# Seven-product W_O in the middle block, with the next block's operands spread over three weight stages, and column sums by transposition

## The chip, the cores and the metric

The kernel runs on one core of one Trainium2 chip. The metric is the device time of one execution in microseconds (us), lower is better. PE is TensorE (matrix products), DVE is VectorE, ACT is ScalarE, POOL is GpSimd and SP is SyncE; SP and POOL issue the DMAs.

## The reference

It is one layer of a hybrid streaming model in float32, for a prompt of 2048 tokens and a decode batch of 64 tokens with a model width D of 1024. Cut to what matters here:

```
h = rms_norm(x, g_pre);  proj = h @ w_in                       # ten outputs of width 1024
vA,bA,cA,zA,q,f,iv,zB,gA,gB = split(proj)
yA = (silu(zA) * bA * conv3(cA * vA)) @ w_a_out                # path A
yB = (norm(gated_linear_attention(q, f, iv)) * silu(zB)) @ w_b_out   # path B, 8 heads
merged = sigmoid(gA) * yA + sigmoid(gB) * yB
out = merged @ w_o
x = x + rms_norm(out, g_post)
x = x + (p @ w_ple_proj) * sigmoid(rms_norm(x, g_ple) @ w_ple_gate)
```

`rms_norm` divides by the root of the mean square over the 1024 features of a token.

## The kernel before, in words

**Blocks.** All 2112 tokens lie in the columns, features in the 128 partitions. Three blocks of 704 tokens (first, middle, last) are worked one after the other, each as two halves of 352 columns, so nearly every matmul has a moving operand of 128x352. Each float32 product is made of three matmuls: weights and activations are split into a high and a low part (`split`: ACT casts the high part, DVE subtracts it for the low part), and high x high, high x low and low x high are added up in PSUM.

**Products.** A product with 2x2 sub-blocks (two column blocks of weights, two token halves) takes 8 sub-products when done plainly. Most stages use seven instead (Strassen's way in Winograd's form): sums S1 to S4 of weight blocks and T1 to T4 of activation blocks are built first, and seven sub-products are combined. `sgroup` does seven products for one pair of weight columns. `in_turn` does one product after the other for all four pairs `g` of a weight matrix: 7 products x 4 pairs x 12 matmuls, 336 in all; while product `n` runs, `prepare` makes the operand of product `n+1` from the raw tiles, and a `sink` takes the finished results. `final_out` (through `gemms`, `gemm_late`, `gemm`, `mm3`) does W_O plainly: 8 columns x 2 halves x 8 row blocks x 3, 384 matmuls.

**Stages of a block.** `path_b` (eight attention heads), `path_a` (gated convolution), then the weight stages W_A, W_B and W_O, then the two norms (`final_norm`) and the last gate. The gate projections of the next block (`gates`) are run while the norms of the block before are worked. In the middle and last block W_A and W_B are `in_turn`. W_O is `in_turn` in the last block alone, and plain in the first two. While the plain W_O runs, `operands` makes the next block's scaled activations (`scaled_x`: x times the row's factor) and their T sums, in four steps.

**Hooks.** Work of other stages is woven in by `hooks`, a list of steps. After each product (12 matmuls) `hook()` takes the next entry and emits it; an entry of `None` emits nothing. `spread_out` fills the list by counts. In `path_b`, the four steps of each head's attention for its three groups of tokens become hooks of the next head's products. For the very first head, six empty hooks stand ahead of them.

**Order.** The program is emitted in that order and then scheduled: each engine's instruction list is fixed when the program is built, and an engine works through its own list in order. Tiles come from pools with fixed numbers of buffers; the largest, `ring`, has 51 buffers for tiles of 704 columns, and `hf` has 9 of 352 columns. `placed` ties an instruction to come after the last matmul emitted so far.

**Column sums.** The mean square of a token is a sum over partitions. `col_rstd` does it with a matmul whose stationary operand is a 128-token piece of the squares and whose moving operand is a column of ones; DVE scales the sums, POOL raises them to the power -1/2, and `spread` broadcasts the result by three transposing matmuls per half:

```
T.matmul(pc[:, i : i + 1], acc[:, o : o + P], ones, start=True, stop=True)   # col_rstd
```

**Weight sums.** `prepare_sums` makes S1 to S4 of W_A and W_B in the first block, of W_O in the middle block and of the last gate in the last block, and stores them with their low parts in DRAM for later stages. In the middle and last block a group's four sums are emitted at once, at the start of an iteration of `path_a`.

Of the kernel before, what the change touches and what calls it, by code (L numbers as in the profile page):

```python
# [18 lines left out]
P = 128  # L19
# [23 lines left out]
LEAD = 7  # L43

# [38 lines left out]
def hybrid_step(  # L83
# [54 lines left out]
    ones = const.tile([P, 1], F32, tag="ones", name="ones")  # L138
    V.memset(ones, 1.0)
# [169 lines left out]
    def prepare_sums(firsts, ahead):  # L309
# [23 lines left out]
        for n, (i1, _) in enumerate(groups):  # L333
            a11, a21, a22, a12 = nxt
            if ahead and n + 1 < len(groups):
                nxt = load(*groups[n + 1])
            V.tensor_tensor(a22, a21, a22, ALU.add)
            keep("S1", i1, a22)
            V.tensor_tensor(a21, a11, a21, ALU.subtract)
            keep("S3", i1, a21)  # L340
            V.tensor_tensor(a11, a22, a11, ALU.subtract)
            keep("S2", i1, a11)
            V.tensor_tensor(a12, a12, a11, ALU.subtract)
            keep("S4", i1, a12)
            if not ahead and n + 1 < len(groups):
                nxt = load(*groups[n + 1])
            yield
# [266 lines left out]
    def col_rstd(acc, n):  # L614

        pc = ps_attn()
        cols = cols_tile(n)
        with placed():
            for i, o in tiles_of(n):
                T.matmul(pc[:, i : i + 1], acc[:, o : o + P], ones, start=True, stop=True)  # L620
        rstd_of(pc[:, : cols.shape[1]], cols, 1.0 / D)
        return cols

    def rms(acc, out, segs, copy=A.copy):


        cols = [col_rstd(acc[:, cols_of(sg)], sg["n"]) for sg in segs]
        yield
        for sg, col in zip(segs, cols):
            copy(out[:, cols_of(sg)], spread(col, sg["n"]))  # L630
        yield

    def sum_squares(j, src, acc, n):
        if j == 0:
            A.activation(acc, src, AF.Square)
        else:
            sq = rt(n)
            A.activation(sq, src, AF.Square)
            V.tensor_tensor(acc, acc, sq, ALU.add)  # L639
# [52 lines left out]
    def scaled_x(xk, k, rs):  # L692
        return V.scalar_tensor_tensor(xk, xk, g_pre[:, k : k + 1], rs, ALU.mult, ALU.mult)  # L693

# [323 lines left out]
    def path_b(bl, hc, first, kept, fills, hs):  # L1018
# [106 lines left out]
    def merge_in_turn(a, kept, mg, made):  # L1125
# [9 lines left out]
        def sink_b(g, c, h, x, y):  # L1135
# [3 lines left out]
            made(j, h)  # L1139
# [32 lines left out]
    def out_in_turn(mg, xo, acc):  # L1172
        xo.extend(rt() for _ in range(KB))
        begun = set()

        def sink(g, c, h, x, y):
            v = half(xo[g + c * KH], h)
            into(v, x, y)
            sum_squares(int(h in begun), v, half(acc, h), HN)
# [172 lines left out]
    with behind_all((*done, *copies)):  # L1352
        cols = [col_rstd(half(acc, h), HN) for h in range(2)]
# [27 lines left out]
    for bi, bl in enumerate(blocks):  # L1381
# [10 lines left out]
        def side(rows, sums_):  # L1392
            for j in range(KB):
                if 1 <= j <= 4:
                    next(rows, None)
                if j >= 3:
                    next(sums_, None)
                yield
# [8 lines left out]
        mg, xo, h2, acc = [], [], [], rt()  # L1407
        if first:
            mg = merge(bl, a, kept, sums_ahead)
        else:  # L1410
            parts = [None] * KB

            def made(j, h):

                if nxt:
                    if parts[j] is None:
                        parts[j] = rt(dt=F32R), rt(dt=F32R)
                    split(half(mg[j], h), *(half(t, h) for t in parts[j]))
# [7 lines left out]
            for idx, n in in_turn(stages, a_first):  # L1426
                loads(idx, n)
                if idx == W_O and n in (0, 2, 3, 5):
                    next(again)
                if (idx, n) == (W_O, 4):  # L1430
                    norms = [final_norm(bl, [s], xo, acc, h2, None, True) for s in segs]
                    spread_out((norms[0], (1, 0, 1, 1, 1, 1, 1, 1)))
            if nxt:
                mg = parts
        if nxt:
            hc = new_operands()
            ops = operands(hc, spread_all(cols), partial(load_x, nxt))
            for j, _ in enumerate(final_out(segs, mg, xo, acc, KB - 1 if first else KH - 1)):
                if j in (1, 3, 5, 7):
                    run(ops, 1)  # L1440
            fills = gates(nxt, hc, kepts[bi + 1], False)
            norm = final_norm(bl, segs, xo, acc, h2, kept, not first)
            spread_out((norm, (0, 1, 0, 1) + (0, 1, 0) * KB + (0, 1, 0, 1) + (0, 1) * KB))
# [63 lines left out]
```

## Time and profile before

| what | value |
|---|---|
| median of 3 runs (lowest, highest) | 2607.93 us (2607.01, 2609.65) |
| the profiled execution | 2607.91 us |
| its span, first to last instruction | 2606.2 us |
| PE busy | 2584.8 us (99%) |
| DVE busy | 1659.5 us (64%) |
| ACT busy | 1532.4 us (59%) |
| POOL busy | 392.3 us (15%) |
| granted PE clock | 1.00 |

The page gives busy time of the engines, not of their queues. A matmul's shown duration overlaps the next one's, so a group's busy time is no price: the price of a matmul is read from how far apart starts lie, or from a stage's length over its count. In a timeline a row holds start, duration, engine, line, operation and the tiles written and read; brackets hold the idle time of the engine just before it and what ended that. In a view by windows each engine has its busy time and, in brackets, its number of instructions.

### The profile page before, as it was taken

Reading aid. Unit: us, or ns where it says so; the run is one execution under the profiler, and the core shown is the slowest. Engines: PE = TensorE matmul, PEld = TensorE weight load, DVE = VectorE, ACT = ScalarE, POOL = GpSimd, SP = SyncE. Lnnn points to the kernel's source line nnn. Section 1 sums busy time; section 2 is a strip of 40 time slices with the busy share of each in tenths; the row PEclk is TensorE's granted clock in tenths of the full one; section 3 lists DMA queues with packets and bytes.
Section 4 is the critical chain, followed back from the end, with each engine's and each line's share of the span. In section 5 each row is a group of like instructions: output and inputs, shape, how many; then the busy total and the mean of one; then the engine's idle time right before and its main releaser. Section 6 shows DMA issues by size and latency. Waiting matters only on the chain. (4 is left out here: it accounts for less than half of the span.)

```text
span 2606.2 us, 47480 instructions
## 1 busy us (share of the span) xinstructions
PE 2584.8 (99%) x16562; PEld 2569.0 (99%) x16562; DVE 1659.5 (64%) x3232; ACT 1532.4 (59%) x2940; POOL 392.3 (15%) x722
## 2 busy tenths in 40 slices
PE   8999999999999999999999999999999999999999
PEld 8999999999999999999999999999999999999998
DVE  8778888898776554455545568553455544568756
ACT  6666665554335645677755556466677744555746
POOL 2000000110431211100112211021000101210220
PEclk9999999999999999999999999999999999999999
DMA  7677787898987998777789989599777779989977
GB/s 289 237 266 262 252 294 256 308 324 290 338 294 275 372 309 271 234 226 227 226 291 354 384 310 307 196 354 358 234 228 225 223 254 339 393 309 309 337 255 238
DMA packets 362672, 745.99 MB, mean 286 GB/s; under 512 B 44640, under 2 KB 49280, under 8 KB 362432
## 3 DMA queue, kind: packets, MB, share of 16 engines
q1 hardware_dynamic: 319680, 579.55, 66.0%
q0 software_dynamic: 42464, 163.37, 17.0%
q8 instruction: 130, 2.13, 0.3%
q14 instruction: 110, 0.90, 0.1%
q10 hardware_dynamic: 288, 0.05, 0.0%
HBM read 531.74 MB, written 211.04 MB: 285 GB/s over the span
## 5 line engine op out<-in xcount | busy, mean ns | idle before, releaser
L363 PE MATMUL pg<-r,hi 128*128 128x352 f32 x3304 | 1091.6, 331 | 1.5 <-DVE r L409 1.0
L364 PE MATMUL pg<-r,hi 128*128 128x352 f32 x3304 | 1067.0, 323 | 0.0
L365 PE MATMUL pg<-r,lo 128*128 128x352 f32 x2356 | 761.9, 323 | 2.1 <-DMA lo<-low 2.0
L218 ACT CAST hi<-raw 128x512 fp32r<-128x512 f32 x720 | 444.4, 619 | 504.7 <-PE pg L364 164.0
L363 PEld LDWEIGHTS pg<-r,hi 128*128 128x128 f32 x3304 | 621.6, 188 | 4.6 <-issue 1.8
L364 PEld LDWEIGHTS pg<-r,hi 128*128 128x128 f32 x3304 | 622.0, 188 | 0.0
L365 PEld LDWEIGHTS pg<-r,lo 128*128 128x128 f32 x2356 | 442.7, 188 | 3.3 <-DMA lo<-low 3.2
L365 PE MATMUL pg<-r,s 128*128 128x352 f32 x948 | 306.5, 323 | 0.0
L529 PE MATMUL pg<-r,hi 128*128 128x352 f32 x768 | 248.4, 324 | 1.1 <-ACT r L188 1.1
L530 PE MATMUL pg<-r,hi 128*128 128x352 f32 x768 | 248.4, 323 | 0.0
L188 DVE TENSOR_TENSOR r<-r,r 128x352 fp32r<-128x352 f32 (+3 forms) x298 | 182.6, 636 | 65.6 <-ACT r L188 64.6
L188 ACT CAST hi<-raw 128x512 fp32r<-128x512 f32 x218 | 134.3, 620 | 148.8 <-PE pg L364 57.1
L497 PE MATMUL pg<-r,hi 128*128 128x352 f32 x672 | 217.2, 325 | 0.1
L496 PE MATMUL pg<-r,hi 128*128 128x352 f32 x672 | 213.4, 325 | 0.2 <-ACT r L188 0.2
L531 PE MATMUL pg<-r,lo 128*128 128x352 f32 x656 | 212.0, 323 | 0.0
L188 ACT CAST r<-r 128x352 fp32r<-128x352 f32 (+3 forms) x298 | 161.9, 578 | 47.0 <-DVE r L693 12.8
L188 DVE TENSOR_TENSOR lo<-raw,hi 128x512 fp32r<-128x512 f32 x218 | 148.7, 686 | 58.5 <-PE pg L531 24.2
L365 PEld LDWEIGHTS pg<-r,s 128*128 128x128 f32 x948 | 178.1, 188 | 0.3 <-DMA s<-low 0.3
L377 ACT COPY hf<-pg 128x352 f32<-128x352 f32 x354 | 157.0, 446 | 7.9 <-PE pg L365 7.1
L188 ACT CAST hi<-s 128x512 fp32r<-128x512 f32 x160 | 97.9, 617 | 93.5 <-PE pg L364 67.7
L529 PEld LDWEIGHTS pg<-r,hi 128*128 128x128 f32 x768 | 144.1, 188 | 1.4 <-ACT r L188 1.4
L530 PEld LDWEIGHTS pg<-r,hi 128*128 128x128 f32 x768 | 144.3, 188 | 0.5 <-DVE r L188 0.3
(367 smaller groups left out, 4150.5 us busy)
## 6 DMA issues: line engine op xcount, KB each, us to landing
raw<-w_blk SPq DMA_DIRECT2D x570, 256.0 KB, 4.3
lo<-low SPq DMA_DIRECT2D x411, 256.0 KB, 4.4
raw<-S SPq DMA_DIRECT2D x408, 256.0 KB, 4.5
low<-lo SPq DMA_DIRECT2D x314, 256.0 KB, 3.6
s<-low SPq DMA_DIRECT2D x309, 256.0 KB, 4.3
S<-s SPq DMA_DIRECT2D x152, 256.0 KB, 3.2
r<-w_blk POOLq DMA_DIRECT2D x64, 256.0 KB, 6.9
S<-r POOLq DMA_DIRECT2D x64, 256.0 KB, 5.9
```

Of the source, the lines that this page charges most:

```text
L188: return A.copy(hi, src).ins, V.tensor_tensor(lo, src, hi.bitcast(F32), ALU.subtract).ins
L218: A.copy(hi, raw)
L363: add(hi[:, k, :], xhi, start=start and k == 0, stop=False)
L364: add(hi[:, k, :], xlo, start=False, stop=False)
L365: last[0] = add(lo[:, k, :], xhi, start=False, stop=k == KH - 1).ins
L377: copied = A.copy(got[n], ps[bank])
L496: add(hi[:, k, :], xhi, start=start and k == 0, stop=False)
L497: add(hi[:, k, :], xlo, start=False, stop=False)
L529: T.matmul(ps, hi[:, k % 4, :], xhi[:, c], start=k == ks[0], stop=False)
L530: T.matmul(ps, hi[:, k % 4, :], xlo[:, c], start=False, stop=False)
L531: last[0] = T.matmul(ps, lo[:, k % 4, :], xhi[:, c], start=False, stop=k == ks[-1]).ins
```

## The change

**Middle block's W_O.** It goes through `in_turn` as a third stage behind W_A and W_B, with 336 matmuls in place of 384. The early split of the merged activations (`made`) is gone; `prepare` makes the operands. `out_in_turn` takes its tiles as they are needed. The low parts of W_O that no one reads any more aren't stored in the first block.

**Next block's operands.** `operands_in_steps` does for the middle block what `operands` did, in 33 steps instead of 4; 29 of them are hooks of the 84 products of W_A, W_B and W_O, at the places in `STEPS_AT`, and four are emitted behind W_O. The first block keeps the plain W_O and `operands`.

**Column sums.** `col_rstds` transposes each 128-token piece by an identity (three 128x128 transposes per half), and DVE adds up along the free axis; one scaling and one power then serve both halves.

**Weight sums singly.** In the middle and last block each sum S1 to S4 is a hook of its own.

**Smaller edits.** The first head's six empty hooks become three ahead of the first attention step and three ahead of the third. In the gates that carry `final_norm`, the broadcast stands one hook further behind the column sums. Squares of half tiles go to the `hf` pool.

The program has 15,834 matmuls instead of 15,882: 48 fewer of 128x352; 42 column-sum matmuls become 42 transposes.

```diff
+STEPS_AT = (0, 8, 9, 10, 12, 13, 14, 15, 20)
+STEPS_AT += (28, 29, 37, 40, 41, 42, 49, 53)
...
-                unread = W_A <= idx < W_O and (idx % KB < KH or half_ == 0)
+                unread = half_ == 0 and W_O <= idx < W_G and idx % KB >= KH
+                unread = unread or W_A <= idx < W_O and (idx % KB < KH or half_ == 0)
...
+                V.tensor_tensor(out, x, y, op)      # prepare_sums, over S1, S3, S2, S4
+                keep(name, i1, out)
+                if not ahead:
+                    yield
...
-    def col_rstd(acc, n):
-        pc = ps_attn()
-        cols = cols_tile(n)
-        with placed():
-            for i, o in tiles_of(n):
-                T.matmul(pc[:, i : i + 1], acc[:, o : o + P], ones, start=True, stop=True)
-        rstd_of(pc[:, : cols.shape[1]], cols, 1.0 / D)
-        return cols
+    def col_rstds(accs, n):
+        nt = len(tiles_of(n))
+        cols = small.tile([P, nt * len(accs)], F32, tag=f"colsum{len(accs)}", name=nm("colsum"))
+        parts = [cols[:, i * nt : (i + 1) * nt] for i in range(len(accs))]
+        for acc, part in zip(accs, parts):
+            pc = ps_attn()
+            with placed():
+                for i, o in tiles_of(n):
+                    T.transpose(pc[:, i * P : i * P + P], acc[:, o : o + P], ident)
+            V.tensor_reduce(part, cols3(pc, nt), axis=mybir.AxisListType.X, op=ALU.add)
+        rstd_of(cols, cols, 1.0 / D)
+        return parts
...
-            sq = rt(n)
+            sq = hf() if n == HN else rt(n)
...
+    def operands_in_steps(hc, cols, load):
+        rs = spread_all(cols)
+        asked = [load(0), load(KH)]
+        yield
+        for i in range(KH):
+            pair = asked
+            for x, k in zip(pair, (i, i + KH)):
+                scaled_x(x, k, rs)
+                yield
+            (b11, b12), (b21, b22) = ([half(x, h) for h in range(2)] for x in pair)
+            s, t = rt(), rt()
+            hc["B11"].append(narrow(b11))
+            V.tensor_tensor(half(s, 0), b12, b11, ALU.subtract)
+            V.tensor_tensor(half(s, 1), b22, b12, ALU.subtract)
+            yield
+            V.tensor_tensor(half(t, 0), b22, half(s, 0), ALU.subtract)
+            V.tensor_tensor(half(t, 1), b21, half(t, 0), ALU.subtract)
+            yield
+            for sums_, lower, upper in ((s, "T1", "T3"), (t, "T2", "T4")):
+                hi, lo = split_rt(sums_)
...
+                yield
+            hi, lo = split_rt(pair[1])
...
+            yield
+            if i + 1 < KH:
+                asked = [load(i + 1), load(i + 1 + KH)]
+            yield
...
-            hooks.extend([None] * 6 if first and hd == 0 else [])
-            for step in range(4):
+            wait = 3 if first and hd == 0 else 0
+            for before in (wait, 0, wait, 1):
+                hooks.extend([None] * before)
                 hooks.extend(partial(next, g) for g in attn)
-                if step == 2:
-                    hooks.append(None)
...
-            stages, loads = merge_in_turn(a, kept, mg, made)
-            if not nxt:
-                stages.append(out_in_turn(mg, xo, acc))
+            stages, loads = merge_in_turn(a, kept, mg)
+            stages.append(out_in_turn(mg, xo, acc))
+            if nxt:
+                hc = new_operands()
+                ops = operands_in_steps(hc, cols, partial(load_x, nxt))
+                counts = [0] * (3 * 7 * KH)
+                for at in STEPS_AT:
+                    counts[at] += 1
+                spread_out((ops, counts))
...
-            spread_out((norm, (0, 1, 0, 1) + (0, 1, 0) * KB + (0, 1, 0, 1) + (0, 1) * KB))
+            spread_out((norm, (0, 1, 0, 0, 1) + (0, 1, 0) * (KB - 1) + (0, 1) + (0, 1, 0, 0, 1) + (0, 1) * KB))
```

**What moves, first place: DVE in the middle block's W_O.** Before, this is the list from the start of the plain W_O (L693 is `scaled_x`, L675 to L678 the T sums, L188 the split, L639 the adding up of squares; `vec` holds the weights of the norm):

```order
L639 TENSOR_TENSOR r_19083<-r_19083,r_20710 128x704
L693 SCALAR_TENSOR_TENSOR r_20713<-r_20713,vec,r_20568 128x704
L693 SCALAR_TENSOR_TENSOR r_20716<-r_20716,vec,r_20568 128x704
L188 TENSOR_TENSOR r_20719<-r_20713,r_20719 128x352
L675 TENSOR_TENSOR r_20722<-r_20713 128x352
L676 TENSOR_TENSOR r_20722<-r_20716,r_20713 128x352
```

Now, from the sixth of W_O's seven products on, with the same work at L704, L719 to L723 and L192 (L416 and L524 are the sinks, which read PSUM or add up products, L650 adds up squares):

```order
L192 TENSOR_TENSOR r_21232<-r_20060,r_21232 128x352
L524 TENSOR_TENSOR r_20630<-r_20630,hf_21167 128x352
L704 SCALAR_TENSOR_TENSOR r_21144<-r_21144,vec,r_19102 128x704
L416 TENSOR_TENSOR r_21057<-r_20630 128x352
L704 SCALAR_TENSOR_TENSOR r_21146<-r_21146,vec,r_19102 128x704
L650 TENSOR_TENSOR r_20703<-r_20703,hf_21171 128x352
L524 TENSOR_TENSOR r_20655<-r_20655,hf_21196 128x352
L192 TENSOR_TENSOR r_21305<-r_21144,r_21305 128x352
L416 TENSOR_TENSOR r_21083<-r_20655 128x352
L719 TENSOR_TENSOR r_21303<-r_21144 128x352
L416 TENSOR_TENSOR r_20704<-r_20606,pg_21123 128x352
```

The operand steps moved from a stage in which DVE only added up squares to one in which they stand between sinks; the last of the four pairs of loaded x tiles (r_21144, r_21146) is scaled there.

**Second place: DVE in the first head's attention of the first block.** L874 to L879 are the second head's keys, L977 and L980 the first head's running states, which PE's next attention product reads. Before:

```order
L874 TENSOR_TENSOR hf_1350<-r_1148,r_1342 128x384
L188 TENSOR_TENSOR lo_1614<-raw_1605,hi_1613 128x512
L875 TENSOR_TENSOR r_1351<-r_1148,r_1342 128x2x128
L876 TENSOR_TENSOR r_1351<-r_1148,r_1342 128x192
L878 TENSOR_TENSOR r_1351<-hf_1350,qc_1349 128x2x2x64
L879 TENSOR_TENSOR r_1351<-hf_1350,qc_1349 128x64
L977 COPY r_1503<-pa_1498 128x128
L383 TENSOR_TENSOR hf_1434<-hf_1434,pg_1508 128x352
L188 TENSOR_TENSOR lo_1624<-s_1619,hi_1623 128x512
L980 SCALAR_TENSOR_TENSOR r_1503<-r_1503,qc_960,pa_1498 128x128
```

Now (L1020 and L1023 are the states, L887 and L889 the second head's scan, which stands ahead of its keys):

```order
L1020 COPY r_1365<-pa_1360 128x128
L1023 SCALAR_TENSOR_TENSOR r_1365<-r_1365,qc_957,pa_1360 128x128 x2
L192 TENSOR_TENSOR lo_1428<-raw_1389,hi_1427 128x512
L1023 SCALAR_TENSOR_TENSOR r_1365<-r_1365,qc_957,pa_1360 128x128
L1023 SCALAR_TENSOR_TENSOR one_1466<-r_1365,qc_957,pa_1464 128x128
L887 SCALAR_TENSOR_TENSOR r_1371<-keep,r_1370 128x704
L192 TENSOR_TENSOR lo_1434<-raw_1387,hi_1433 128x512
L889 TENSOR_TENSOR r_1370<-r_1371 128x704
```

The states moved from behind the second head's keys to ahead of its scan.

**Third place: DVE in the middle block's `path_a`, at a group of weight sums.** L337 to L343 are S1, S3, S2 and S4; L388, L383 and L409 combine products out of PSUM. Before:

```order
L337 TENSOR_TENSOR r_17371<-r_17370,r_17371 128x512
L339 TENSOR_TENSOR r_17370<-r_17369,r_17370 128x512
L388 TENSOR_TENSOR hf_17452<-hf_17452,hf_17467 128x352
L341 TENSOR_TENSOR r_17369<-r_17371,r_17369 128x512
L383 TENSOR_TENSOR hf_17437<-hf_17437,pg_17469 128x352
L343 TENSOR_TENSOR r_17372<-r_17372,r_17369 128x512
```

Now (L348 is each of the four sums, L395 and L390 the combinations):

```order
L348 TENSOR_TENSOR r_17358<-r_17357,r_17358 128x512
L348 TENSOR_TENSOR r_17357<-r_17356,r_17357 128x512
L395 TENSOR_TENSOR hf_17439<-hf_17439,hf_17454 128x352
L348 TENSOR_TENSOR r_17356<-r_17358,r_17356 128x512
L390 TENSOR_TENSOR hf_17424<-hf_17424,pg_17456 128x352
L348 TENSOR_TENSOR r_17359<-r_17359,r_17356 128x512
```

Nothing moved here: the four sums stand in the same places between the same combinations.

More of the change, by code (lines that the diff above doesn't have):

```diff
@@ L1123, in merge, with merge_in_turn @@
         return mg
-    def merge_in_turn(a, kept, mg, made):
+    def merge_in_turn(a, kept, mg):
         ob, m = [], []
@@ L1172, in out_in_turn @@
     def out_in_turn(mg, xo, acc):
-        xo.extend(rt() for _ in range(KB))
+        xo.extend([None] * KB)
         begun = set()
         def sink(g, c, h, x, y):
-            v = half(xo[g + c * KH], h)
+            j = g + c * KH
+            if not acc:
+                acc.append(rt())
+            if xo[j] is None:
+                xo[j] = rt()
+            v = half(xo[j], h)
             into(v, x, y)
-            sum_squares(int(h in begun), v, half(acc, h), HN)
+            sum_squares(int(h in begun), v, half(acc[0], h), HN)
             begun.add(h)
@@ L1352, in hybrid_step @@
     with behind_all((*done, *copies)):
-        cols = [col_rstd(half(acc, h), HN) for h in range(2)]
+        cols = col_rstds([half(acc, h) for h in range(2)], HN)
         ph, done = split_p(ph1)
@@ L1395, in side @@
                     next(rows, None)
-                if j >= 3:
+                if j == 3:
                     next(sums_, None)
+                elif j > 3:
+                    hooks.extend(partial(next, sums_, None) for _ in range(5))
                 yield
@@ L1406, in hybrid_step @@
             next(sums_ahead)
-        mg, xo, h2, acc = [], [], [], rt()
+        mg, xo, h2, acc = [], [], [], [rt()] if first else []
         if first:
@@ L1410, in hybrid_step @@
         else:
[L1411 to L1418, printed above, removed]
-            stages, loads = merge_in_turn(a, kept, mg, made)
-            if not nxt:
-                stages.append(out_in_turn(mg, xo, acc))
+            stages, loads = merge_in_turn(a, kept, mg)
[7 more added lines that the diff above has]
+                spread_out((ops, counts))
+            else:
                 rows2 = []
@@ L1427, in hybrid_step @@
                 loads(idx, n)
+                if nxt:
+                    continue
                 if idx == W_O and n in (0, 2, 3, 5):
```

43 lines of the change are left out of this document (23 added, 20 removed).

## Prediction

> **What bounds the kernel now.** The page comes first: who is busy, and for how much of the span.
>
> ```profile
> span 2606.2 us, 47480 instructions
> PE 2584.8 (99%) x16562; PEld 2569.0 (99%) x16562; DVE 1659.5 (64%) x3232; ACT 1532.4 (59%) x2940; POOL 392.3 (15%) x722
> ```
>
> PE is busy for 99%, so the time is PE's own work and what PE waits for, 21.4 us in all. The profiled execution took 2607.91 us, 1.7 us more than its span, and lies 0.02 us from the median of 2607.93. The sum is therefore made against 2607.91. The view of waits, for PE alone, says where PE stood (us in total, times, longest):
>
> ```profile
> PE pa L1063 <- ACT r L188: 6.6, 1, 6.6
> PE pg L365 <- DMA lo<-low: 2.0, 3, 1.7
> PE pa L999 <- DVE r L980: 1.4, 1, 1.4
> PE pg L529 <- ACT r L188: 1.1, 1, 1.1
> PE pg L363 <- DVE r L409: 1.0, 2, 0.6
> ```
>
> The first is the start of the program, which the change doesn't touch. Three others lie where the change works: the first head (L999), the step from W_B to the plain W_O (L529) and `path_a` with its weight sums (L363). Removed waits can give 3.5 us at most, so a larger gain must come out of PE's work. That is priced by stages. Each row of the view by windows is a stretch, its length, then busy time of PE, PEld, DVE, ACT and POOL with their counts, the granted clock, the DMA share and GB/s: the middle block's W_A and W_B, its plain W_O, then the last block's W_A and W_B, and its W_O by seven products.
>
> ```profile
> 1516.26:1625.76 109.50, 109.50 (x674) 107.95 (x673) 83.32 (x179) 67.40 (x143) 11.73 (x23) 1.00 0.88 302
> 1626.33:1689.90 63.57, 62.44 (x387) 61.73 (x386) 34.69 (x56) 30.11 (x56) 4.76 (x9) 1.00 0.59 193
> 2299.56:2408.62 109.06, 108.95 (x674) 108.07 (x673) 86.54 (x182) 65.05 (x137) 10.62 (x20) 1.00 0.90 306
> 2408.62:2464.72 56.10, 55.95 (x346) 54.87 (x346) 38.92 (x81) 41.41 (x87) 11.39 (x21) 1.00 0.95 326
> ```
>
> The reader sees the new stage already running, in the last block: the same matrix with the same 336 matmuls takes 56.10 us there, against 63.57 for the plain 384.
>
> **W_O of the middle block: 8.3 us less.** The last block's 56.10 us also hold nine records of a norm, six of column sums and three of a broadcast, which the next fence prices.
>
> ```profile
> 2451.34 0.72 PE L620 MATMUL pa<-ones,r 128*128 128x1 f32 x6
> 2451.92 0.41 PE L498 MATMUL pg<-r,s 128*128 128x352 f32 x1
> 2454.59 0.49 PE L604 MATMUL pa<-ident,cols 128*128 128x128 f32 x3
> 2454.84 0.41 PE L496 MATMUL pg<-r,hi 128*128 128x352 f32 x1
> ```
>
> From start to next start the six take 0.58 us and the three 0.25. So W_O alone is 56.10 - 0.83 = 55.3 us, and 63.57 - 55.3 = 8.3 us go. The fast end is the pace of W_A and W_B, 109.50/2 = 54.75 us (8.8 us less); the slow end is under the density of DVE below. The 1.1 us wait at L529 lies inside the 63.57. It arose because the plain W_O needed whole split tiles at once. W_O's first product needs only first halves, which W_B's second product finishes, so nothing is late next there. At the other end four steps are emitted behind W_O. They are three splits, and the next gates need them only after 36 matmuls; 3 x 0.89 us (row below) lie under 36 x 0.16 = 5.8 us. I put that at nothing; without that cover it costs up to 2.7.
>
> **Column sums: 4.0 us less, 0.5 more at the start.** One half's sums cost 0.58 us by ones and should cost 0.25 by transposes, which the broadcast's transposes of the same shape show: 0.33 less. There are 14 halves. Twelve lie in stages that PE bounds: 12 x 0.33 = 4.0 us. The start's own rows, below, give 1.25 for twelve records and 0.70 for six, 0.27 a half: 3.3 us, the lower bound. The other two halves are in the start, where PE waits for a chain through DVE and POOL:
>
> ```profile
> 20.16 1.39 PE L620 MATMUL pa<-ones,r 128*128 128x1 f32 x12
> 21.41 0.41 PE L1063 MATMUL pa<-r,r 128*128 128x352 f32 x1
> 23.42 0.87 PE L604 MATMUL pa<-ident,cols 128*128 128x128 f32 x6
> 24.12 0.43 PE L1063 MATMUL pa<-r,r 128*128 128x352 f32 x1
> 20.92 0.16 DVE L591 TENSOR_SCALAR cols<-pa 128x3 f32<-128x3 f32 x1 [0.31 <-PE pa L620]
> 22.06 1.69 DVE L188 TENSOR_TENSOR r<-r,r 128x704 fp32r<-128x704 f32 x2 [0.32 <-issue]
> 22.64 1.05 POOL L593 TENSOR_TENSOR cols<-cols,mhalf 128x3 f32<-128x3 f32 x1
> L1006 DVE TENSOR_REDUCE ms<-r x24: 679/686/687, 126.3 to 2096.6; 128x4 f32<-128x512 f32 x24
> L1006 DVE TENSOR_REDUCE ms<-one x24: 276/279/283, 127.4 to 2100.7; 128x1 f32<-128x128 f32 x24
> ```
>
> No row shows a reduction of 3x128 out of PSUM; between 0.28 us for 128 and 0.69 for 512 elements it is about 0.55. Two of them follow the transposes: from about 20.7 to 21.8. In DVE's new list one of the two splits (1.69/2 = 0.85) then stands ahead of the scaling: to 22.6. The scaling (0.16) and POOL's power (1.05), with 0.2 between each, end at 24.0, so the broadcast starts near 24.2 in place of 23.42. That is up to 0.8 us later; if the chain is hidden, PE gains 1.25 - 0.70 = 0.55. I take 0.5 later, nearer to the end that the list gives. In the gates the broadcast now has a hook more, and in the last block the first has 24 matmuls (3.9 us) for a chain of about 2.6, so the later ones cost nothing.
>
> The rule that speaks against this edit is in the Trainium skill, TensorE: Matmul & The Clock Gate, Part 4: a transpose through TensorE took about 275 ns in a kernel, and it doesn't count as work that keeps the clock up. By it the 42 transposes would be 11.6 us, an estimate, and the sum 2603.4. The trace agrees with 275 as a duration and not as a price, and shows a clock of 1.00 in each stage above.
>
> **First head: 1.35 us less.** PE's L999 stood for the running states:
>
> ```profile
> 121.11 0.71 PE L999 MATMUL pa<-r,att 128*128 128x128 f32 x4 [1.35 <-DVE r L980]
> ```
>
> They stood behind the second head's keys in DVE's list and now stand ahead of its scan, while L999 keeps its hook, the thirteenth. What is moved past them is needed only a head later. The first transposes come three hooks earlier, but their keys were done 15 us before. Bounds: 1.35 less, or nothing if the states are late for another reason.
>
> **Weight sums singly: nothing.** In DVE's list they haven't moved, and what they wait for isn't each other:
>
> ```profile
> 1420.04 0.69 DVE L337 TENSOR_TENSOR r<-r,r 128x512 f32<-128x512 f32 x1 [6.43 <-DMA r<-w_blk]
> ```
>
> DVE idles 6.43 us for their load, and then all four are ready. The bounds are 1.0 us less (the wait at L363) and nothing.
>
> **Operand steps in W_A to W_O: 0.6 us more.** These are prices on DVE (busy, mean ns), from the middle block:
>
> ```profile
> L693 DVE SCALAR_TENSOR_TENSOR r<-r,vec,r 128x704 f32<-128x704 f32 x8 | 7.5, 945 | 0.0
> L675 DVE TENSOR_TENSOR r<-r 128x352 f32<-128x352 f32 x4 | 2.1, 524 | 0.2
> L188 DVE TENSOR_TENSOR r<-r,r 128x704 fp32r<-128x704 f32 x9 | 7.7, 889 | 2.9 <-ACT r L188 2.8
> L188 DVE TENSOR_TENSOR r<-r,r 128x352 fp32r<-128x352 f32 x63 | 31.7, 520 | 5.8 <-ACT r L188 5.4
> ```
>
> One pair of x tiles costs 2 x 0.945 + 0.52 + 4 x 0.52 + 3 x 0.89 = 7.2 us of DVE. Two pairs fall into W_A and W_B: 14.4, and 2.1 for the first operand of W_O; the 16 early splits go, 8.3. DVE's 83.3 us become 91.5 of 109.5, 84%. The last block runs the same stage at 86.5 of 109.06 and loses nothing, so the lower bound is nothing. The upper bound, 1.5 us, is what the last W_O loses against the pace (55.3 - 54.55 by 109.06/2 = 0.75), twice. W_O gets a pair and two thirds of another, 11.7 us: at most 38.9 + 11.7 = 50.6 of 56.1, 90%. If that paces the late products PE loses about 2 us there, my slow end. I take 0.6 for the whole.
>
> The eight loads of x go past POOL's reloads of gates and heads, and the scalings at L704 wait for them with sinks and operand splits queued behind on DVE, and PE behind those. I put it at nothing: the last pair is issued 33 matmuls (5.3 us) ahead, and issue and landing take 0.54 + 4.2 us:
>
> ```profile
> r<-x_fm POOLq DMA_DIRECT2D x12, 352.0 KB, 4.2
> L643 POOL DMA_DIRECT2D r<-x_fm x8 | 4.3, 537 | 84.9 <-DVE r L188 27.5 <-PE pg L531 23.9 <-DVE r L639 20.9
> r<-g__3190_13221 POOLq DMA_DIRECT2D x1, 352.0 KB, 8.6
> ```
>
> **The sum.** 2607.91 - 8.3 - 4.0 + 0.5 - 1.35 + 0.6 = 2595.4 us.
>
> **Rival one, slower: x lands late.** The fence above shows POOL standing up to 27.5 us for a free buffer at L643, and a reload landing in 8.6 us. The ring now also holds the operands while `in_turn` runs. If each pair is issued only when DVE is at L704, DVE stands 2 x 0.54 + 8.6 = 9.7 us; PE has nine matmuls (1.45 us) of cover before the fourth operand is missing. Four pairs cost 4 x 8.2 = 33 us: 2628. It turns the sign when PE loses over 17.7/4 = 4.4 us a pair. Against it: the pairs are asked four or eight hooks (7.7 or 15 us) ahead. Chance 0.05.
>
> **Rival two, no change: DVE's idle time can't be filled.** If DVE's 26.2 us idle in W_A and W_B and 17.2 in W_O are waits that stay, the added 8.2 and 11.7 us lengthen the stages by 19.9; with half of it the time is 2605.4. The chain of ACT and DVE (2.8 and 5.4 us of waits at L188) speaks for it, the last block's fuller and shorter stage against it. Chance 0.06.
>
> **Rival three: a transpose costs its shown duration.**
>
> ```profile
> L604 PE MATMUL pa<-ident,cols 128*128 128x128 f32 x54 | 7.8, 273 | 0.0
> ```
>
> Then 42 x 0.273 = 11.5 us stand in place of 14 x 0.25 = 3.5: 2603.4. The row's 7.8 us for 54, 0.14 each, speak against it. Chance 0.03. This is the Trainium skill's figure of Part 4 taken as a price.
>
> **How the numbers follow.** The forecast has 0.86, and 2595.4 is its time. Its best case is 8.8 + 4.0 + 0.55 + 1.35 + 1.0 = 15.7 less, 2592.2. Its worst is 6.3 + 3.3 - 0.8 - 1.5 = 7.3 less, 2600.6. The range is 2591 to 2602, a little beyond both for what no row shows. About 0.2%, 5.2 us, is what a measurement can tell: below 2602.7 is faster. Faster is 0.86, within 0.2% 0.09 (rivals two and three), slower 0.05.
>
> **What would show it.** The middle block's W_O should last 55 to 56 us at 336 matmuls, and the two stages ahead of it about 110. L999 should have no wait for the running states. A half's column sums should be 0.25 us on PE, and the broadcast at the start should come after 24 us. The pair of waits in `path_a` for the combinations should stay. The prediction is wrong if PE shows waits on operand splits in W_A to W_O of more than 3 us together, if DVE stands at L704 for DMAs, or if the gates behind W_O begin with a wait.

## The result and the profile after

The changed kernel takes 2602.31 us (median of eight runs, 2598.71 to 2603.89) beside 2607.13 us of the kernel before: a ratio of 0.998, 95% interval 0.997 to 0.9989. A second series gave 2602.33 against 2607.77, 0.9981 (0.9972 to 0.999). So about 5 us are gained where 12.5 were forecast, and 2602.3 lies just outside the range of 2591 to 2602. The profiled execution took 2599.16 us, at the fast end of its eight runs. That matters below, for its trace does not show the largest loss.

First the page of the changed kernel, span and busy times. PE's busy time fell from 2584.8 to 2572.1 us, 12.7 us less:

```profile
span 2597.5 us, 47426 instructions
PE 2572.1 (99%) x16472; PEld 2558.2 (98%) x16472; DVE 1686.6 (65%) x3295; ACT 1545.2 (59%) x2972; POOL 391.0 (15%) x717
```

The view of waits of PE, in the columns that the prediction used:

```profile
PE pa L1105 <- ACT r L192: 6.7, 1, 6.7
PE pa L611 <- POOL colsum L600: 5.3, 4, 2.2
PE pg L538 <- DVE lo L192: 1.3, 1, 1.3
PE pg L370 <- DVE r L416: 1.3, 2, 0.7
```

The first head's wait and the one between W_B and W_O are gone. The pair in `path_a` has stayed. New is the second row: the broadcast (L611) waits for POOL's power (L600) in four places, 5.3 us in all: 1.6 at the start, 0.3 and 1.2 in the gates behind the first and the middle block, 2.2 in the last gate. Before, it waited for POOL nowhere.

The view by windows, for W_A and W_B of the middle block and then for its W_O by seven products:

```profile
1515.95:1626.25 110.30, 109.89 (x679) 108.63 (x679) 96.41 (x201) 70.27 (x147) 12.76 (x24) 1.00 0.92 321
1626.25:1680.96 54.71, 54.71 (x338) 54.02 (x337) 44.86 (x94) 41.89 (x90) 3.23 (x6) 1.00 0.89 286
```

W_O takes 54.71 us in place of 63.57, and PE stands in neither window for more than 0.4 us. The six transposes of the next block's broadcast now stand inside the first window. Two signs of being wrong that the prediction names do show, but small: DVE stood once at L704 for a tile of x, 1.0 us, without PE standing for it, and 2.6 us into the gates behind W_O PE stood 0.6 us for a load, which the second profile doesn't have. Otherwise this part did what the prediction said.

At the start, the timeline of the changed kernel (start, length, engine) shows the chain behind the column sums:

```profile
21.07 0.82 PE L630 MATMUL pa<-ident,r 128*128 128x128 f32 x6
25.56 0.87 PE L611 MATMUL pa<-ident,colsum 128*128 128x128 f32 x6 [1.60 <-POOL colsum L600]
21.59 1.02 DVE L631 TENSOR_REDUCE colsum<-pa 128x3 f32<-128x384 f32 x2
22.53 0.88 DVE L192 TENSOR_TENSOR r<-r,r 128x704 fp32r<-128x704 f32 x1
23.33 0.17 DVE L598 TENSOR_SCALAR colsum<-colsum 128x6 f32<-128x6 f32 x1
23.58 1.92 POOL L600 TENSOR_TENSOR colsum<-colsum,mhalf 128x6 f32<-128x6 f32 x1 [1.03 <-DVE colsum L598]
```

The split that stands ahead of the scaling is there, as read from the list. But the power over six columns takes 1.92 us where I had put 1.05. The broadcast comes at 25.56, not at 24.2, and the first product of the first block at 76.74, not at 74.60. Only a part of these 2.1 us belongs to the edit. In this profile the column sums themselves begin 0.9 us later, at 21.07 for 20.16, behind the same 72 matmuls; in the 17 traces they begin anywhere from 20.16 to 21.65. From the first column sum to the broadcast it is 3.26 us by ones and 4.49 by transposes, within 0.02 in every trace. So the edit costs 1.2 us at the start, where I had 0.5.

### The profile page after: what moved, and what is told of

It is laid out like the page before. It is cut to its first block, busy times and chain, and to the rows that moved or that the text cites. A ratio compares the mean times of both kernels' runs of the same rounds, so it can differ in the third digit from the quotient of the medians.

```text
span 2597.5 us, 47426 instructions
## 1 busy us (share of the span) xinstructions
PE 2572.1 (99%) x16472; PEld 2558.2 (98%) x16472; DVE 1686.6 (65%) x3295; ACT 1545.2 (59%) x2972; POOL 391.0 (15%) x717
## 5 line engine op out<-in xcount | busy, mean ns | idle before, releaser
L372 PE MATMUL pg<-r,lo 128*128 128x352 f32 x2356 | 761.9, 323 | 1.4 <-DMA lo<-low 1.4
L222 ACT CAST hi<-raw 128x512 fp32r<-128x512 f32 x732 | 452.0, 619 | 491.6 <-PE pg L371 167.6
L370 PEld LDWEIGHTS pg<-r,hi 128*128 128x128 f32 x3304 | 622.2, 188 | 3.7 <-issue 1.8
L371 PEld LDWEIGHTS pg<-r,hi 128*128 128x128 f32 x3304 | 622.3, 188 | 0.0
L192 DVE TENSOR_TENSOR r<-r,r 128x352 fp32r<-128x352 f32 (+3 forms) x306 | 187.3, 633 | 59.0 <-ACT r L192 58.7
L192 ACT CAST hi<-raw 128x512 fp32r<-128x512 f32 x218 | 134.1, 619 | 151.1 <-PE pg L371 59.4
L538 PE MATMUL pg<-r,lo 128*128 128x352 f32 x584 | 188.6, 323 | 1.3 <-DVE lo L192 1.3
L192 ACT CAST r<-r 128x352 fp32r<-128x352 f32 (+3 forms) x306 | 165.4, 576 | 37.8 <-DVE r L704 10.3
L192 DVE TENSOR_TENSOR lo<-raw,hi 128x512 fp32r<-128x512 f32 x218 | 148.9, 687 | 57.7 <-PE pg L538 21.6
L505 PE MATMUL pg<-r,lo 128*128 128x352 f32 x504 | 162.5, 323 | 0.0
L192 ACT CAST hi<-s 128x512 fp32r<-128x512 f32 x160 | 98.0, 617 | 97.9 <-PE pg L371 72.0
L504 PEld LDWEIGHTS pg<-r,hi 128*128 128x128 f32 x784 | 147.5, 188 | 3.1 <-DVE r L192 2.5
```

Of the source, the lines that this page charges most:

```text
L192: return A.copy(hi, src).ins, V.tensor_tensor(lo, src, hi.bitcast(F32), ALU.subtract).ins
L222: A.copy(hi, raw)
L370: add(hi[:, k, :], xhi, start=start and k == 0, stop=False)
L371: add(hi[:, k, :], xlo, start=False, stop=False)
L372: last[0] = add(lo[:, k, :], xhi, start=False, stop=k == KH - 1).ins
L504: add(hi[:, k, :], xlo, start=False, stop=False)
```

## The experiments

Every kernel below ran beside the kernel before on the same chip. Ratios are to that kernel, with their 95% intervals; one thousandth is 2.6 us. The chips differ from group to group. The first four runs take the parts one by one.

**Column sums by ones again, all else as changed.**

```diff
-        cols = col_rstds([acc[:, cols_of(sg)] for sg in segs], segs[0]["n"])
+        cols = [col_rstd(acc[:, cols_of(sg)], sg["n"]) for sg in segs]
...
-(0, 1, 0, 0, 1) + (0, 1, 0) * (KB - 1) + (0, 1) + (0, 1, 0, 0, 1) + (0, 1) * KB
+(0, 1, 0, 1) + (0, 1, 0) * KB + (0, 1, 0, 1) + (0, 1) * KB
```

> The changed kernel with the old column sums (by ones, a power of its own for each half, the old hooks). Theory: the transposes take 4.6 us off PE, and the waits for POOL's power at the broadcast (5.3 us in four places) and a later start give more than that back; stage by stage the traces put the edit at +2.2 us (start +2.1, gates behind the middle block +0.35, last gate +0.65, the rest -0.9). So this kernel should be some 2.2 us below the changed one, 9 to 11 below the kernel before, with no wait at the broadcast over 0.3 us outside the start. Rival (the prediction's term): the edit gains 3.5 net, and this kernel is about 3.5 above the changed one.

Measured: 2606.44 us, ratio 0.9994 (0.9985 to 1.0003). It is slower than the changed kernel by 4 (the two intervals just overlap), so the theory, which had it 2.2 faster, fell, and the prediction's term stood, in this kernel. In its trace the broadcast of the last gate waits 1.8 us for POOL although the sums are made by ones: that wait isn't the transposes'.

**Column sums by transposition alone, on the kernel before.** The same edit the other way round.

> The kernel before with column sums by transposition alone (and the hook more ahead of the broadcast). Theory: 1 to 2.5 us slower than the kernel before; the start 2 us later, and waits for POOL at the broadcast of 4 us or more in all. Rival (the prediction's term): 3.5 us faster.

Measured: 2606.97 us, 0.9997 (0.9988 to 1.0006). Neither 3.5 faster nor slower by more than 1.6. The start is later, as the theory had it, but the waits at the broadcast are 2.8 us in all and not 4.

**First head's hooks alone, on the kernel before.**

```diff
-            hooks.extend([None] * 6 if first and hd == 0 else [])
-            for step in range(4):
+            wait = 3 if first and hd == 0 else 0
+            for before in (wait, 0, wait, 1):
+                hooks.extend([None] * before)
```

> The kernel before with the first head's steps at their new hooks alone; lows are stored as before. PE should come out of the first block's products about 3.1 us earlier (the wait at the combination, 1.35, and two stalls behind ACT near 193 us, 1.3, go). Theory: the plain W_O behind it is paced by transfers of its weights, whose last split comes at the same time as before; PE then stands there some 2 to 3 us at the low parts, and the whole gains 0 to 1 us. Rival: what made that wait in the changed kernel is that lows are no longer stored, so here there is none and 3.1 us are gained.

Measured: 2607.70 us, 0.9999 (0.999 to 1.0008). The first block's products took 576.5 us against 578.9, but no wait at the low parts appeared behind them: the theory's mechanism is not there. The median shows no gain.

**W_O in turn and the operand steps alone, on the kernel before.** The changed kernel with column sums, first head, weight sums and stored lows as before; squares of half tiles in `hf`, as the change has them.

> The kernel before with W_O of the middle block by seven products and the next operands in steps alone (column sums by ones, first head, weight sums and stored lows as before). Theory: the three stages take 165.0 us in place of 173.7 as in the changed kernel, and behind them nothing is given back: 8 to 9 us faster. Rival (the prediction's sum, with a charge of 0.6 for DVE's density): 7.7 faster. Second rival: the gates behind begin late, as in the changed kernel (0.8), and 7.5 to 8 are left.

Measured: 2608.34 us, 1.0003 (0.9994 to 1.0011). No gain at all, though the three stages took 164.40 us against 173.72. Two rows of the trace show where 8 to 9 us went. One warns against reading a single profile too finely. Until 1516 us this kernel's instructions are those of the kernel before, in the same order, and still the first block's W_A to W_O differ, here before and then this kernel:

```profile
653.52:839.76 186.24, 186.23 (x1160) 185.91 (x1159) 132.62 (x209) 77.35 (x133) 66.61 (x124) 1.00 0.85 304
```

```profile
654.31:843.59 189.28, 186.68 (x1161) 185.80 (x1160) 132.72 (x209) 77.08 (x133) 66.48 (x124) 1.00 0.84 299
```

Three microseconds from one run to another, out of waits for loaded weights. The +1.3 at L538 in the changed kernel is of this kind. The other is the last gate, behind the last block's W_O: 71.08 us against 65.45, and 71.0 in the kernel with sums by ones. In the three kernels with the middle W_O plain it was 65.3 to 65.5. The first profile of the changed kernel had shown 66.10 there.

**The changed kernel once more.**

> The changed kernel once more, beside the kernel before on this chip. Theory: what one profile shows in the stages that are fed by loads (start, first block's W_A to W_O, last W_O and gate) moves by 1 to 3 us from run to run with the same instructions, since the kernel with W_O in turn alone, whose instructions are those of the kernel before up to 1516 us, was 2.3 us later there; so this profile should differ from the first one by 1 to 3 us in such stages, and by less than 0.5 in the middle block's three stages (165.0). The median should be 2601 to 2603.5, 4 to 6 below before. Rival: the 2599.16 of the first profile is typical, and the median lies within 1 of it.

Measured: 2602.33 us, 0.9981. Its last gate took 70.36 us, so 66.10 was the exception. The windows of the last gate, before and in this run:

```profile
2464.82:2530.27 65.45, 64.97 (x413) 64.63 (x412) 47.48 (x91) 26.48 (x55) 15.74 (x26) 1.00 0.79 278
```

```profile
2453.10:2523.46 70.36, 65.82 (x405) 64.89 (x403) 47.34 (x91) 26.12 (x54) 13.48 (x21) 0.98 0.73 255
```

PE's waits in that window of the second run, and ACT's timeline there (in brackets what the engine waited for):

```profile
PE pa L611 <- POOL colsum L600: 2.9, 1, 2.9
PE pa L630 <- DVE r L650: 1.7, 1, 1.7
```

```profile
2453.04 0.62 ACT L222 CAST hi<-raw 128x512 fp32r<-128x512 f32 x1 [2.20 <-DMA raw<-w_blk]
2453.56 0.49 ACT L649 ACTIVATE hf<-r 128x352 f32<-128x352 f32 x1
2457.25 0.62 ACT L222 CAST hi<-raw 128x512 fp32r<-128x512 f32 x1 [3.19 <-DMA raw<-w_blk]
2457.77 0.88 ACT L649 ACTIVATE hf<-r 128x352 f32<-128x352 f32 x2
```

The gate's weights are late. ACT stands in its list at their splits (L222), with the squares (L649) behind; DVE's adds wait for the squares, the column sums for the adds (1.7), the broadcast for what follows (2.9). The two loads at which ACT stands were asked for 10 and 9 us ahead of the gate in both kernels. From issue to landing (the last number, a median of the two) they took 6.9 us before and 11.2 now:

```profile
raw<-w_blk SPq DMA_DIRECT2D x2, 256.0 KB, 6.9
raw<-w_blk SPq DMA_DIRECT2D x2, 256.0 KB, 11.2
```

So they landed 3.7 and 1.5 us ahead of the gate before, and 0.2 us ahead and 4.0 behind now. ACT's list has another order, too (before, four splits stand together; now a square stands behind each of these two), but with the old landings neither split would have waited. What the loads met on their way, POOL's timeline shows. Here it is before, with the gate beginning at 2464.82:

```profile
2462.36 1.07 POOL L1042 DMA_DIRECT2D r<-p_fm  x2 [2.19 <-DVE r L188]
2463.82 0.54 POOL L1086 DMA_DIRECT2D r<-x  x1 [0.39 <-PE pg L498]
...
2479.75 0.60 POOL L1086 DMA_DIRECT2D r<-x  x1
2480.35 0.54 POOL L1086 DMA_DIRECT2D r<-p  x1
```

And here in the second run of the changed kernel, with the gate beginning at 2453.10:

```profile
2444.42 1.08 POOL L1084 DMA_DIRECT2D r<-p_fm  x2
2445.49 0.55 POOL L1128 DMA_DIRECT2D r<-x  x1
...
2451.61 0.55 POOL L1128 DMA_DIRECT2D r<-x  x1 [0.33 <-PE pg L505]
2452.77 0.55 POOL L1128 DMA_DIRECT2D r<-p  x1 [0.61 <-DVE r L416]
```

Before, POOL waited for free tiles (`r`) and asked for `p_fm` 2.5 us ahead of the gate; now 8.7 us ahead. The second pair of `x` and `p`, 352 KB each, used to go out 15 us behind the gate's start and now goes out just ahead of it. In POOL's list that pair stood behind the power on the last gate's column sums, and now stands ahead of it: the freed tiles have changed the list as well as the waits. These transfers share the DMA engines with the gate's weights: in the 7 us ahead of the gate the engines moved 389 GB/s, against 306 before. That the free tiles come from the smallest of the edits, squares of half tiles that no longer take a tile of the ring, is the reading that the next experiments try.

**Three more parts undone.** The low parts stored as before, the weight sums four at a time, the first head's hooks as before:

```diff
-                unread = half_ == 0 and W_O <= idx < W_G and idx % KB >= KH
-                unread = unread or W_A <= idx < W_O and (idx % KB < KH or half_ == 0)
+                unread = W_A <= idx < W_O and (idx % KB < KH or half_ == 0)
```

> The changed kernel with the low parts of W_O's first halves stored as before. Theory: the wait for a low part in the first block's plain W_O (1.3) isn't made by that edit, since two kernels that store them had it as well (1.3 and 2.6), and the time is the changed kernel's within 1 us. Rival one: the edit makes the wait, and this kernel is 1.3 faster. Rival two: four stores of 256 KB less, in a stretch where the DMA engines are busy for 0.83 to 1.00 of the time, let the weights land earlier, and this kernel is 1 to 3 us slower.

> The changed kernel with the weight sums four at a time, as before. Theory (the prediction's): within 0.5 us of the changed kernel. Rival: sums singly smooth what DVE and POOL do in path_a of the middle and the last block (waits at the combination of 2 to 3 us in all in each of the traces), and this kernel is 1.5 to 3 us slower.

> The changed kernel with the first head's steps at their old hooks. Theory: the first block's products take 1.4 to 3.1 us more, and the plain W_O behind them gives that back, since it waits for loads: within 1 us of the changed kernel, as the edit alone gave nothing on the kernel before. Rival (the prediction): 1.35 or more slower.

Measured, beside 2602.33: lows stored 2600.85 (0.9971, 0.9961 to 0.9982), sums grouped 2603.18 (0.9981, 0.9972 to 0.999), old hooks 2603.86 (0.9985, 0.9977 to 0.9994). All within 1.6 us of the changed kernel, with intervals that overlap: none of the three is what is missing. Their last gates took 69.2, 70.2 and 70.2 us.

**Squares of the last block in the ring again.**

```diff
-            sq = hf() if n == HN else rt(n)
+            sq = hf() if own and n == HN else rt(n)
```

`own` is false in the last block.

> The changed kernel with the half squares of the last block in ring buffers again, as in the kernel before (the change puts them into the small half buffers). Theory: the last gate takes 70.2 us in the kernels with the middle W_O in turn and 65.3 in the others, because the ring now has free buffers some 5 us earlier there, and POOL asks nine to eleven tiles (p, x, gates' x) ahead of the gate's weights instead of behind them; the weights then land late, ACT's splits wait, the squares behind them, and the column sums and the broadcast wait 2.0 and 3.2 us, with a slow clock for about 1.2 us behind. With the squares in the ring POOL stands again, the gate takes 65 to 66, and the time falls by 4 to 5: 2597.5 to 2598.5. Rival: the ring is free earlier because W_O's output tiles and the sum's are taken only when needed, and this kernel is the changed one within 1 us. Second rival: the squares' adds on DVE are late by themselves, and nothing changes either.

Measured: 2596.37 us (2595.72 to 2598.91), 0.9957 (0.9944 to 0.9969), 5.9 below the changed kernel, with intervals that lie apart. The last gate took 64.66 us, POOL stands for tiles again, and the two loads of weights, asked for 11 and 9 us ahead of the gate, landed after 7.7 us (last row):

```profile
2453.20:2517.86 64.66, 64.18 (x403) 63.54 (x403) 48.89 (x94) 26.92 (x55) 15.56 (x26) 1.00 0.80 281
```

```profile
2450.74 1.09 POOL L1084 DMA_DIRECT2D r<-p_fm  x2 [2.18 <-DVE r L192]
...
2468.22 0.60 POOL L1128 DMA_DIRECT2D r<-x  x1
...
raw<-w_blk SPq DMA_DIRECT2D x2, 256.0 KB, 7.7
```

**Last block's output tiles taken early.**

```diff
-        xo.extend([None] * KB)
+        xo.extend(None if nxt else rt() for _ in range(KB))
```

> The changed kernel with the last block's eight output tiles and the sum's tile taken ahead of the stage, as before, and the squares in half buffers as in the changed kernel. Theory (squares): the last gate stays at 69 to 71, the time within 1 us of the changed kernel. Rival (tiles taken late): the gate falls to 65 to 66, the time by 4 to 5.

Measured: 2601.16 us, 0.9977 (0.9965 to 0.9988), last gate 69.0 us. The late tiles are not the cause.

**Half squares alone, on the kernel before.**

```diff
-            sq = rt(n)
+            sq = hf() if n == HN else rt(n)
```

> The kernel before with squares of half tiles in half buffers, nothing else. Theory: POOL's loads of the next stage go out some 5 us earlier in the last block, the gate's weights land late, and the last gate takes 69 to 71 in place of 65.4: 4 to 6 us slower than the kernel before. Rival: it needs the middle block's other order as well, and this kernel is within 1 us of the kernel before.

Measured: 2612.26 us, 1.002 (1.0011 to 1.0029): 5.1 us slower by this line alone (2.9 to 7.6), with a plain W_O. The instructions of PE, DVE, ACT and POOL are those of the kernel before up to the last block's W_O. The two loads of weights took 11.3 us there, and the gate 4.2 us more than before. The window of its last gate and PE's waits in it are those of the changed kernel:

```profile
2467.24:2536.86 69.62, 65.18 (x413) 64.59 (x412) 46.26 (x88) 25.61 (x54) 13.79 (x20) 1.00 0.74 254
```

```profile
PE pa L604 <- POOL cols L593: 3.3, 1, 3.3
PE pa L620 <- DVE r L639: 1.2, 1, 1.2
```

**W_O in turn alone, half squares of the last block in the ring.**

> The kernel before with the middle W_O in turn alone, the last block's half squares in the ring. Theory (the prediction's terms, 8.3 less and 0.6 more): 7 to 9 below the kernel before, last gate 65 to 66. Rival: the stage's gain is given back elsewhere too (loads, slow clock behind a wait), and only 4 to 5 come.

Measured: 2601.15 us, 0.9978 (0.9969 to 0.9987): 6 us faster, 3.4 to 8.1. The three stages take 165.15 us, the last gate 65.2. The gain of the stage is there once that line is out; the prediction's 7.7 lies in the interval. The stages are 8.6 us shorter, but the last block's gates and products 2.0 longer (611.53 against 609.58), with a wait of 1.4 us for a loaded low part.

**Column sums by ones, half squares in the ring.**

> The changed kernel with the last block's half squares in the ring and the column sums by ones. Theory: the transposes' 4 us on PE are eaten by the waits at the broadcast and the later start, and this kernel is 0 to 2 us below the one with transposes (2596.4 there). Rival (the prediction): 3.5 us above it.

Measured: 2599.93 us, 0.9972 (0.9961 to 0.9984), 3.6 above the kernel with transposes (the intervals overlap, as in the first such pair, which gave the same size). The theory fell again. Where the 3.6 arise, the two traces show in the last block's gates and products: 614.74 us by ones, 609.89 by transposes. By ones, one wait stands there, and the clock falls behind it (the last two rows: the wait, then what follows it):

```profile
PE pg L374 <- DMA lo<-low: 2.9, 1, 2.9
```

```profile
1678.09:2292.83 614.74, 611.87 (x3974) 610.28 (x3973) 298.52 (x597) 371.78 (x690) 80.78 (x149) 1.00 0.85 290
1705.60:1708.80 3.20, 0.34 (x3) 0.05 (x1) 2.96 (x5) 1.59 (x4) 1.60 (x3) 1.00 1.05 401
1708.80:1713.20 4.40, 4.39 (x18) 4.39 (x19) 0.52 (x1) 1.81 (x4) 0.73 (x2) 0.61 1.02 375
```

The same stretch with transposes:

```profile
1678.90:2288.79 609.89, 608.01 (x3961) 606.30 (x3961) 300.42 (x599) 371.61 (x690) 80.56 (x147) 1.00 0.86 292
```

```profile
PE pa L611 <- POOL colsum L600: 1.2, 1, 1.2
```

PE waits for POOL instead, 1.2 us, and keeps the clock. The four traces with the middle W_O in turn and sums by ones have 611.5 to 614.7 us for these gates and products, the nine with W_O in turn and transposes 608.8 to 610.2. What makes that load late by ones was not tried. On the kernel before there is no such wait to remove, which goes with the edit's giving nothing there.

**Cover for the chain, and both together.** The start's sums by ones and two powers, as before, and one hook more between column sums and broadcast in the gates:

```diff
-        cols = col_rstds([half(acc, h) for h in range(2)], HN)
+        cols = [col_rstd(half(acc, h), HN) for h in range(2)]
...
-(0, 1, 0, 0, 1) + (0, 1, 0) * (KB - 1) + (0, 1) + ...
+(0, 1, 0, 0, 0, 1) + (0, 1, 0) * (KB - 2) + (0, 1) * 2 + ...
```

> The changed kernel with the start's column sums by ones and two powers, as before, and one hook (24 matmuls, 3.9 us) more between column sums and broadcast in the gates behind the first and the middle block. Theory: transposes pay where the chain of reductions, scaling and power has cover: the start gets 1.5 to 2 us back, the waits at the broadcast in the gates (0.5 and 1.4) go, and the time is 3 to 4 below the changed kernel. Rival: what is ahead there is lost at the next load, and less than 1.5 is gained.

> Both of these together: squares of the last block in the ring, the start by ones, a hook more ahead of the broadcast. Theory: the two add, 7 to 8.5 below the changed kernel: 2594 to 2595.5. Rival: they share the same time, and 4 to 5 are gained.

Measured: 2598.29 us (0.9962, 0.9949 to 0.9974) and, with the squares in the ring, 2594.47 us (0.995, 0.9937 to 0.9962). The first gains 4 on the changed kernel, with intervals that just touch; in its profile 2.0 of them lie in the last gate, where a wait of 2.9 us at the broadcast was followed by no slow clock, so not all of it is the cover's. The second beats both kernels, 12.8 us below before; over the ring alone it gains 1.9, with intervals that overlap.

## Why the prediction was wrong, point by point

- **W_O of the middle block: right.** 54.71 us against 55.3, and W_O's first product waits for nothing.
- **Operand steps: right in mechanism, the charge too high.** DVE was fuller in W_A and W_B than reckoned (95.5 to 96.4 us, not 91.5) and emptier in W_O (44.9 to 45.8, not 50.6), and it cost PE 0.4 us. The one wait for x, 1.0 us of DVE, held nothing up: rivals one and two fell.
- **Column sums: the price right, "the later ones cost nothing" wrong.** Six transposes take about 0.6 us on PE, as forecast, and rival three fell. But the broadcast then waits, 0.3 and 1.2 us in the gates behind the first and the middle block, where both halves go through one power. There the chain of two reductions (1.0), scaling and power (1.4 and 1.6) stands behind adds in DVE's list. The wait in the last gate is another matter, as it stands with sums by ones as well. On the chip the edit is worth nothing that can be measured on the kernel before and about 4 us in the changed one, where a load's wait goes as well. That the size of 3.5 net was met there is luck: it came by a way that I had not named.
- **The start: mis-sized.** 1.2 us more, not 0.5. The power over six columns was priced by the power over three.
- **First head: right in the trace, not seen in the times.** L1042 has no wait for the running states, and the products take 576.5 us with the new hooks against 578.9. The medians (0.4 us slower alone at a ratio of 0.9999, 1.5 faster inside the change) do not resolve 1.35.
- **Weight sums singly: right,** nothing that can be measured.
- **The step that failed is one that the prediction does not have.** Half squares in the `hf` pool were an edit of one line, and I gave it no term: in the sum it stands at nothing, without a reason. It costs 5.1 us alone, and taking it out of the last block moves the changed kernel from 2602.3 to 2596.4, which is 5.9 of the 6.9 us by which the forecast of 2595.4 missed. The prediction asked what a moved step waits for; it did not ask what a freed buffer lets start. It quoted POOL's waits for free tiles for x in the middle block; POOL stood for tiles ahead of the last gate too, and with these waits the gate's weights landed in time. That the rest lies within 1 us of the forecast is in part luck, as terms missed both ways: the three stages gave 8.7 us and not 7.7, and the start and the broadcasts in the gates cost 2.3 us more than the sum had.

What stays open: by the measured parts, W_O in turn with half squares in `hf` should take 2607.1 - 6.0 + 5.1 = 2606.2 us, and it measured 2608.3, a difference that the intervals of some 2 us to either side cover. By the forecast of 7.7 it would be 2604.5; of the 3.8 us to that, its trace has 2.0 in the last block's gates and products, as the same kernel with squares in the ring has. The rest can't be told from the 3 us by which the same instructions differ between runs.

## What to carry to other kernels

A buffer that comes free earlier is a transfer that starts earlier: for every edit that changes which pool a tile comes from, look for the queue that stood for that pool, and for what its transfers will then collide with. An edit of one line needs its own term like the large ones. Where loads feed a stage, one profile of each kernel can mislead by 3 us, so a stage that decides is read in two or three runs.

## What the runs showed of the hardware

A standing PE can cost more than the wait. In the repeated run of the changed kernel PE stood 2.9 us at the broadcast (3.2 from start to start), and the matmuls behind it ran at half speed (start to start 0.293 us for 0.161):

```profile
2467.60:2470.80 3.20, 0.38 (x3) 0.08 (x1) 2.43 (x6) 0.50 (x1) 1.47 (x2) 0.96 0.06 19
2470.80:2473.10 2.30, 2.27 (x9) 2.27 (x10) 1.33 (x3) 0.00 (x0) 1.08 (x2) 0.50 0.45 132
```

In ten such places in the 17 traces 7 to 11 matmuls were slow, and 0.9 to 1.5 us were lost. It happened after six of the eight start-to-start gaps of 3.2 us or more, after three of the eight of 2.0 to 2.6 us (the first profile's 2.5 at the same broadcast was not among them), and once below that, behind three gaps in a row. The Trainium skill, TensorE: Matmul & The Clock Gate, Part 1, says that the clock is set by a free-running window of about 3.4 us; the granted clock, which stood at 0.50 for 3.4 us each of the ten times, and the same gap with and without a slow stretch, agree with it.

POOL's power on a few columns took 0.88 to 2.69 us in these traces: in the last gate 0.88 with the squares in the ring and 1.45 without, for the same three columns. Spans on POOL are rough, but PE's waits followed them; what sets them was not tried.
